# Layer 0's last output projection: seven half-depth products per pair of row blocks on two of three column chunks

## The chip, the cores and the metric

The kernel runs on one core of a Trainium2 chip. The metric is the time of one execution on the device in microseconds (us). Five engines matter: TensorE (PE: the matmuls, and PEld: their weight loads), VectorE (DVE), ScalarE (ACT), GpSimd (POOL) and SyncE (SP), which issues most of the DMAs. Each engine runs its own instructions in the order of the program and waits on semaphores for the others.

## The reference, cut to what matters

The program is one inference step of a two-layer decoder trunk over 1024 prompt tokens and 32 sample tokens (1056 columns in all). Layer 0 is a recurrent block, layer 1 a gated linear recurrence.

```
xn = rmsnorm(x); u = xn @ w_in                  # layer 0, 1024 -> 2 * 1536
xb, gate = u[..., :1536], u[..., 1536:]
h  = rg_lru(causal_conv(xb))                    # recurrence over the tokens
y  = h * silu(gate)                             # 1536 rows
x1 = x + y @ w_out                              # 1536 -> 1024: the change is in here
...
layer 1 begins with rmsnorm(x1)                 # so it needs every row of x1 in a column
```

## The kernel before

Activations lie with the features on the 128 partitions and the 1056 tokens along the columns, cut into three chunks of 352 columns (0, 1, 2). Every f32 matrix product is made in three matmuls (`mm3`, L245 to L249): each operand is split into a high part that the PE's reduced f32 form holds exactly and a low part with the rest, and high x high, high x low and low x high are summed in PSUM. ACT makes a high part by a cast, DVE or POOL makes a low part by a subtraction. A block of weights is 128x128, so one block on one chunk costs three matmuls of 128x352.

The 1536 rows of y come in four groups of three blocks. `out(g)` adds the product of groups 0 and 1 to x in DRAM. The last two groups are taken together by `out_last` (L660): for every chunk and each of the eight row blocks m of the result it forms one product over six blocks of y, three of group 2 (`ycols`, the tiles yh and yl) and three of group 3 (`xcols`, the tiles xh and xl). That is 18 matmuls to one PSUM bank; a DVE addition (L710) then adds x, a DMA writes the row block of x1, ACT squares it and POOL adds the squares (`squares`). After the eight blocks of a chunk, `norm` sums the squares over the partitions by a small matmul, POOL takes the power, DVE writes a diagonal and a second matmul spreads the factor; `scaled_parts` (L470, L471, L335) then makes layer 1's high and low parts. The norm and the scaling of chunk c run while the PE is on chunk c+1, those of chunk 2 while the PE is on the first products of layer 1 (`first1`).

The weights of `out_last` stay in the core for all three chunks. `load` fetches them by 128x384 pieces into the small tiles wraw, ACT casts (L670), POOL subtracts (L671), and the parts lie in room that has become free: row block 4 in the gate tiles gh and gl, row blocks 0 to 3 in X (the inputs of the recurrence), 5 to 7 in the last 256 columns of xh and xl and in the tiles whi and wlo.

What y needs first: the last gate products, two row blocks on three chunks (`gate(3, (1, 2), True)`, the DVE lines L534 and L535), and `split_y` (L627 to L632), which makes the high and low parts of groups 2 and 3 by an ACT cast and a DVE subtraction with two inputs in SBUF.

The order of the work is not written out by hand. All operations of the layer go as a list into `Flow`, which holds a duration for each, plans them forwards and backwards, and emits every engine's instructions in the planned order. Operations marked `main` keep their written order on the PE. On the chip the emitted order is fixed.

## Time and profile before

| what | value |
|---|---|
| median of 3 runs | 1046.37 us (1045.69 to 1050.2) |
| profiled execution: time, span of its instructions | 1044.86 us, 1043.1 us |
| mean granted TensorE clock | 0.997 |
| PE busy, matmuls | 98% of the span, 10264 |
| DVE, ACT, POOL busy | 73%, 65%, 48% |

A row of the timeline gives the start in us from the span's first instruction, the busy time, the engine, the line of the kernel, the operation, the output and inputs by the program's names, and how many were merged ("x2"); in square brackets stands the idle time before it and what ended that. The recorded busy times of two neighbours overlap a little, so the pitch of a run is the distance of the starts. `out_last` begins on the PE at 413.68 us.

### The profile page before, as it was taken

To read this page: it belongs to the slowest core of one execution; us is meant where nothing else is said; L and a number is where in the kernel's file an instruction comes from. 1 tells how busy PE (TensorE), PEld (TensorE's weight loads), DVE (VectorE), ACT (ScalarE), POOL (GpSimd) and SP (SyncE) were. 2 spreads that over 40 slices of the span, in tenths; PEclk is the share of its full clock that TensorE was granted. 3 is DMA by queue.
4 is the path that set the end of the run, shared out by engine and by line. 5 is a ranking of instruction groups with operands and counts; after the bars stand their busy time and mean duration, and the time that the engine had idled before them with its cause. 6 is when DMAs were issued, how large, how long until landed. Compare 5 with 4: busy or idle time off the path is not lost.

```text
span 1043.1 us, 26196 instructions
## 1 busy us (share of the span) xinstructions
PE 1027.3 (98%) x10264; PEld 1006.9 (97%) x10264; DVE 756.4 (73%) x1465; ACT 678.6 (65%) x1534; POOL 501.7 (48%) x526
## 2 busy tenths in 40 slices
PE   9999999999999999999999999999999999999996
PEld 9999999999999999999999999999999999999995
DVE  7999997788888599346687555554657567899656
ACT  6568656966865776333468686767777685786444
POOL 3425343444535265645754555555545353244554
PEclk9999999999999999999999999999999999999998
DMA  9201112123752586435676666566567571765554
GB/s 306 64 16 58 54 48 74 41 73 87 228 185 59 154 278 195 152 104 188 209 185 158 124 153 126 145 125 164 120 150 185 137 183 65 227 180 122 108 112 167
DMA packets 90764, 143.71 MB, mean 138 GB/s; under 512 B 11152, under 2 KB 56592, under 8 KB 90640
## 3 DMA queue, kind: packets, MB, share of 16 engines
q1 hardware_dynamic: 74656, 112.46, 34.2%
q0 software_dynamic: 13680, 26.81, 15.2%
q10 hardware_dynamic: 2304, 2.77, 0.8%
q8 instruction: 80, 1.31, 0.5%
q14 instruction: 44, 0.36, 0.1%
HBM read 81.60 MB, written 33.05 MB: 110 GB/s over the span
## 4 chain that ended last, share of the span: by engine, by line
PE 91%; DVE 5%; DMA 2%; issue 1%; POOL 0%; ACT 0%; POOLq 0%; ACTq 0%; DVEq 0%
PE mm L247 26%; PE mm L248 25%; PE mm L249 25%; PE hg L1063 2%; PE hg L1174 1%; PE hg L1281 1%; PE hg L579 1%; PE hg L1235 1%; PE hg L1283 1%; PE hg L247 1%; PE hg L248 1%; PE hg L249 1%; DMA wraw<-in_w_dram 1%; PE hg L1325 1%; DVE R L445 1%
## 5 line engine op out<-in xcount | busy, mean ns | idle before, releaser
L247 PE MATMUL mm<-xh,whi 128*128 128x352 f32 (+1 forms) x1147 | 353.8, 308 | 1.8 <-DVE sg L1543 1.8
L248 PE MATMUL mm<-xl,whi 128*128 128x352 f32 (+1 forms) x1147 | 348.6, 304 | 0.0
L249 PE MATMUL mm<-xh,wlo 128*128 128x352 f32 (+1 forms) x1147 | 348.4, 304 | 0.0
L247 PEld LDWEIGHTS mm<-xh,whi 128*128 128x128 f32 x1147 | 215.5, 188 | 4.1 <-DVE sg L1543 2.2
L248 PEld LDWEIGHTS mm<-xl,whi 128*128 128x128 f32 x1147 | 215.7, 188 | 1.5 <-DVE xl L335 0.2
L249 PEld LDWEIGHTS mm<-xh,wlo 128*128 128x128 f32 x1147 | 215.6, 188 | 0.0
L335 POOL TENSOR_TENSOR wlo<-wraw,whi 128x512 fp32r<-128x512 f32 (+1 forms) x62 | 89.9, 1458 | 82.8 <-ACT whi L390 74.2
L247 PE MATMUL mm<-t,whi 128*128 128x264 f32 x408 | 118.3, 290 | 0.0
L249 PE MATMUL mm<-t,wlo 128*128 128x264 f32 x408 | 115.8, 284 | 0.5 <-POOL wlo L335 0.5
L248 PE MATMUL mm<-t,whi 128*128 128x264 f32 x408 | 115.7, 284 | 0.0
L511 DVE SCALAR_TENSOR_TENSOR k<-xb,prm_sb,k 128x352 f32<-128x352 f32 (+2 forms) x144 | 90.0, 636 | 11.0 <-ACT k L508 7.8
L247 PEld LDWEIGHTS mm<-t,whi 128*128 128x128 f32 x408 | 76.8, 188 | 0.9
L249 PEld LDWEIGHTS mm<-t,wlo 128*128 128x128 f32 x408 | 76.6, 188 | 0.7 <-POOL wlo L335 0.7
L248 PEld LDWEIGHTS mm<-t,whi 128*128 128x128 f32 x408 | 76.9, 188 | 0.1
L322 POOL DMA_DIRECT2D wlo<-wraw x52 | 45.5, 874 | 64.6 <-ACT wlo L321 44.9
L1543 DVE TENSOR_TENSOR k<-mm,k 128x264 f32<-128x264 f32 x72 | 30.7, 429 | 58.7 <-PE mm L249 55.3
L594 POOL TENSOR_TENSOR k<-X 128x352 f32<-128x352 f32 x36 | 43.7, 1224 | 48.0 <-DVE R L595 38.8
L322 POOL DMA_DIRECT2D wlo<-R x32 | 29.4, 926 | 45.1 <-ACT wlo L321 36.5
L247 PE MATMUL mm<-yh,whi 128*128 128x352 f32 x153 | 49.9, 326 | 0.0
L249 PE MATMUL mm<-yh,wlo 128*128 128x352 f32 x153 | 49.4, 323 | 0.0
L248 PE MATMUL mm<-yl,whi 128*128 128x352 f32 x153 | 49.4, 323 | 0.0
L390 ACT CAST whi<-wraw 128x512 fp32r<-128x512 f32 (+1 forms) x63 | 36.3, 591 | 20.0 <-DMA wraw<-in_w_dram 7.7
(425 smaller groups left out, 2680.8 us busy)
## 6 DMA issues: line engine op xcount, KB each, us to landing
wraw<-in_w_dram SPq DMA_DIRECT2D x88, 256.0 KB, 3.3
wlo<-wraw POOLq DMA_DIRECT2D x49, 256.0 KB, 4.1
wlo<-R POOLq DMA_DIRECT2D x30, 256.0 KB, 4.1
wraw<-in_wo_dram SPq DMA_DIRECT2D x37, 192.0 KB, 3.0
ysum<-sg SPq DMA_DIRECT2D x9, 528.0 KB, 5.1
si<-in_s_in_dram SPq DMA_DIRECT2D x8, 512.0 KB, 4.0
R<-in_w_dram SPq DMA_DIRECT2D x16, 256.0 KB, 3.4
out_ss_out_dram<-si SPq DMA_DIRECT2D x8, 512.0 KB, 3.0
```

The costliest lines, as they stand in the source:

```text
L247: T.matmul(out, wh, xh, start=first, stop=False, skip_group_check=chained)
L248: T.matmul(out, wh, xl, start=False, stop=False, skip_group_check=chained)
L249: T.matmul(out, wl, xh, start=False, stop=last, skip_group_check=chained)
L322: fl.add("POOL", 0.93, lambda: G.dma_start(dst.bitcast(F32), src, accum_op=ALU.add), (*r, *w), w, prio, n / 2)
L335: emit = lambda: e.tensor_tensor(b, x, a.bitcast(F32), op=ALU.subtract)
L390: act(m, lambda hi=hi, raw=raw, m=m: S.copy(hi[:, :m], raw[:, :m]), rk, (hk,), prio)
L445: (pool if e is G else dve)(CH, lambda: e.tensor_tensor(a[:, :CH], a[:, :CH], sq, op=ALU.add), (sk, ak), (ak,), 2)
L511: dve(u, lambda src=src, dst=dst, sh=sh, k=k: V.scalar_tensor_tensor(dst, sh(src, k), pc("cw", 12 * k + m), dst, op0=ALU.mult, op1=ALU.add ...
L579: fl.add("PE", 0.62, lambda ps=ps, i=i, c=c: T.matmul(ps[:96, :CH], gs[:, i, :], ST[:96, chunk(c)], start=True, stop=True), (("gs",), *((" ...
L594: pool(CH, lambda x=x, a=a, b=b: G.tensor_tensor(x, a.bitcast(F32), b.bitcast(F32), op=ALU.add), (ak, bk), (xk,), 3)
L1063: T.matmul(ps[32 * j:32 * j + 32, n * w:n * w + w], B[:, o:o + 32], q(slice(o, o + 32)), start=True, stop=True, tile_position=(0, 32 * j))
L1543: dve(QT, lambda: V.tensor_tensor(o[0], z[0], u[0], op=ALU.add), (z[1], u[1]), (o[1],), 0)
```

## The change

On chunks 0 and 1 the eight row blocks are taken as four pairs (m, n) = (0,1), (2,3), (4,5), (6,7). The weights of a pair, two row blocks by two halves of three blocks (11 and 12 for m, 21 and 22 for n), and the y of the two chunks by two groups make a 2x2 by 2x2 product. It is formed by seven products of half the depth (9 matmuls of 128x352 each) in place of eight. The steps, by the kernel's numbers, and where each sum lies in PSUM (a, b, c are three banks of a pair):

```
weights: s = 21 + 22; 21 = 21 - 11; 11 = 11 - s; 12 = 12 + 11        # combos, DVE, four per pair
y: t1 = y2[1]-y2[0]; t3 = y2[1]-y3[1]; t2 = t3-y2[0]; t4 = t2+y3[0]  # difference, DVE, once
step 1: a  = 11 (plain) * y2[0]     step 2: b  = 12 (plain) * y3[0]
step 5: c  = s  * t1                step 3: c += 12 * y3[1]
step 6: a += 11 * t2                step 7: a += 21 * t3
step 4: a += 22 (plain) * t4
```

After each step DVE adds the bank's sum so far to one row block of x1 (L799), so a later step on the same bank has to wait until that addition has read it. On the PE the steps of neighbouring pairs are interleaved: 1 and 5 of the first pair, then for each pair 2, 3, 6, step 1 of the next pair, 7, step 5 of the next pair, 4. In the last pair one plain product of chunk 2 (row block 6) stands between steps 6 and 7, and 7 and 4 follow each other. Then come the other seven products of chunk 2, formed as before. The norms of chunks 0 and 1 are both taken behind the last step.

The weights are now fetched whole, 128x768 a row block, into the tile R (four homes, used twice each), and cast from there (L681, L682). The combined weights and the differences of y are new DVE operations (L733, L759), and their high and low parts new ACT casts (L745, L764) and new DVE subtractions (L746, L765). Chunk 1 of group 2 is no longer split by itself, since only t1 is used of it.

```
-        def split_y(g):
-            for c in range(NCH):
+        def split_y(g, cs=range(NCH)):
+            for c in cs:
...
+            def combos(m, n):
...
+                both_("s", "21", "22", ALU.add)
+                both_("21", "21", "11", ALU.subtract)
+                both_("11", "11", "s", ALU.subtract)
+                both_("12", "12", "11", ALU.add)
+                return at_
+
+            def split(i, p):
+
+                (hi, hk), (lo, lk) = spot[p]
+                x, xk, kx = made[i][{5: "s", 3: "12", 6: "11", 7: "21"}[p]]
+                act(U, lambda: S.copy(hi, x), (xk, *kx), hk, 2)
+                dve(U, lambda: V.tensor_tensor(lo, x, hi.bitcast(F32), op=ALU.subtract), (xk, *kx, *hk), lk, 2, True)
+                return hi, lo, (*hk, *lk)
...
+            def difference(o, x, y, op):
+
+                (o, ok), (x, xk), (y, yk) = o, x, y
+                dve(CH, lambda: V.tensor_tensor(o, x, y, op=op), (xk, yk), (ok,), 2, True)
...
+                for (q, c) in {1: [(m, 0)], 2: [(m, 0)], 5: [(n, 1)], 3: [(m, 1)], 6: [(m, 1)], 7: [(n, 1)], 4: [(n, 0)]}[p]:
+                    if p in (1, 5, 3, 4):
+                        begin_x(q, c)
+                    add(q, c, ps, pk)
+                    if p in (2, 6, 7, 4):
+                        end_x(q, c, accs[c])
...
+            ready(0)
+            step(0, 1)
+            step(0, 5)
+            for i in range(4):
+                if i:
+                    step(i - 1, 4)
+                for p in (2, 3, 6):
+                    step(i, p)
+                if i < 3:
+                    ready(i + 1)
+                    step(i + 1, 1)
+                    step(i, 7)
+                    step(i + 1, 5)
+                else:
+                    whole_(last[0])
+                    step(i, 7)
+                    step(i, 4)
+            for c in range(2):
+                scaled(c, accs[c], range(KD))
+            for m in last[1:]:
+                whole_(m)
+            scaled(2, acc2, last)
...
-        split_y(2)
+        split_y(2, (0, 2))
```

Where the instructions stand now is shown at three places. First the PE at the start of the stage, before: behind the last gate product (bank mm_160) comes the product of row block 4, with weights in gh and gl that were made long ahead; yh0 to yh2 and yl0 to yl2 are group 2, xh and xl group 3.

```order
L249 MATMUL mm_160<-xh_108,wlo_130 128x352
L247 MATMUL mm_157<-yh0_151,gh_116 128x352
L248 MATMUL mm_157<-yl0_154,gh_116 128x352
L249 MATMUL mm_157<-yh0_151,gl_117 128x352
L247 MATMUL mm_157<-yh1_152,gh_116 128x352
L248 MATMUL mm_157<-yl1_155,gh_116 128x352
```

The same place now, from the end of step 1 of the first pair (bank mm_157) into step 5 (bank hg_164), whose weights are the parts whi_125 and wlo_129 of s.

```order
L249 MATMUL mm_157<-yh2_153,X_143 128x352
L247 MATMUL hg_164<-yh0_151,whi_125 128x352
L248 MATMUL hg_164<-yl0_154,whi_125 128x352
L249 MATMUL hg_164<-yh0_151,wlo_129 128x352
L247 MATMUL hg_164<-yh1_152,whi_125 128x352
L248 MATMUL hg_164<-yl1_155,whi_125 128x352
```

So the third matmul of step 5, the twelfth of the stage, reads a low part that DVE makes from s.

The second place is DVE behind the gate products. Before, the last gate product's two operations (L534 on mm_160, L535) were followed by the end of the recurrence, a few low parts and the first additions to x1:

```order
L534 SCALAR_TENSOR_TENSOR k_85<-k_85,mm_160 128x352
L535 SCALAR_TENSOR_TENSOR sg_150<-sg_150,k_85 128x352
L610 TENSOR_TENSOR R_73<-R_73,t0_119 128x8
L611 MEMSET a_113 128x8
L615 SCALAR_TENSOR_TENSOR R_73<-a_113,R_73 128x352
L710 TENSOR_TENSOR sg_146<-mm_157,sg_146 128x352
```

Now the same two are followed by the addition behind step 1 (L799 on mm_157), one difference (L759) and one low part of t1 (L765), and then by these rows:

```order
L759 TENSOR_TENSOR sg_148<-sg_145,sg_148 128x352
L765 TENSOR_TENSOR xl_101<-sg_148,xh_100 128x352
L765 TENSOR_TENSOR yl2_156<-k_85,yh2_153 128x352
L765 TENSOR_TENSOR xl_101<-sg_145,xh_100 128x352
L765 TENSOR_TENSOR xl_107<-sg_148,xh_106 128x352
L759 TENSOR_TENSOR sg_149<-sg_146,sg_149 128x352
L759 TENSOR_TENSOR sg_146<-sg_149,sg_146 128x352
L759 TENSOR_TENSOR sg_149<-sg_146,sg_149 128x352
L765 TENSOR_TENSOR xl_103<-sg_149,xh_102 128x352
L765 TENSOR_TENSOR xl_103<-sg_146,xh_102 128x352
L733 TENSOR_TENSOR R_73<-R_73 128x384
L746 TENSOR_TENSOR wlo_129<-wraw_121,whi_125 128x384
```

The low part of s (the last row) stands behind nine operations on t2, t3 and t4, which only steps 6, 7 and 4 read, and behind a combination of weights.

The third place is the PE at the end of the last pair: step 7 ends and step 4 begins, on the same bank mm_159 (xh_100 to xh_104 hold t3, xh_106 and xh_108 t4).

```order
L247 MATMUL mm_159<-xh_104,whi_126 128x352
L248 MATMUL mm_159<-xl_105,whi_126 128x352
L249 MATMUL mm_159<-xh_104,wlo_130 128x352
L247 MATMUL mm_159<-xh_106,whi_124 128x352
L248 MATMUL mm_159<-xl_107,whi_124 128x352
L249 MATMUL mm_159<-xh_106,wlo_128 128x352
```

Between the two steps there is no other work on the PE; in the earlier pairs step 5 of the next pair stands there. Before, neighbouring products always went to different banks.

More of the change, by code (lines that the diff above doesn't have):

```diff
@@ new lines, in split @@
+            def split(i, p):
[4 more added lines that the diff above has]
+                return hi, lo, (*hk, *lk)
+            t2 = [(xh[3 + j][:, chunk(1)], xl[3 + j][:, chunk(1)], (("xh", 3 + j, 1), ("xl", 3 + j, 1))) for j in range(3)]
@@ new lines, in out_last, with begin_x, add, end_x @@
+            accs = [next(xbs) for _ in range(2)]
+            count = [0, 0, 0]
+            def begin_x(m, c):
+                x, xk = place[m, c]
+                dma(x, src[m][:, chunk(c)], ((2, m, c),), (xk,), 3)
+            def add(m, c, ps, pk):
+                x, xk = place[m, c]
+                dve(CH, lambda: V.tensor_tensor(x, ps[:, :CH], x, op=ALU.add), (pk, xk), (xk,), 0)
+            def end_x(m, c, acc):
+                x, xk = place[m, c]
+                dma(x1d[m][:, chunk(c)], x, (xk,), (("x1d", m, c),), 3)
+                squares(count[c], x, xk, acc)
+                count[c] += 1
@@ new lines, in out_last, with ready @@
+            made = {}
+            def ready(i):
+                keep(two[i][0])
+                keep(two[i][1])
+                made[i] = combos(*two[i])
+            acc2 = next(xbs)
+            ready(0)
[11 more added lines that the diff above has]
+                    step(i + 1, 5)
+                else:
+                    whole_(last[0])
+                    step(i, 7)
+                    step(i, 4)
```

134 lines of the change are left out of this document (99 added, 35 removed).

## The prediction

> **What bounds the kernel now.** I read the page first, its table of busy time and the chain that ended last.
>
> ```profile
> PE 1027.3 (98%) x10264; PEld 1006.9 (97%) x10264; DVE 756.4 (73%) x1465; ACT 678.6 (65%) x1534; POOL 501.7 (48%) x526
> PE 91%; DVE 5%; DMA 2%; issue 1%; POOL 0%; ACT 0%; POOLq 0%; ACTq 0%; DVEq 0%
> ```
>
> The PE is busy nearly always and is 91% of the chain. So a matmul less is time gained, as long as nothing makes the PE wait. Next the stretches before and in the stage that changes (windows, 394 to 414, 414 to 456 us):
>
> ```profile
> core 0: us, PE busy (x) PEld busy (x) DVE busy (x) ACT busy (x) POOL busy (x), PEclk, DMA share, GB/s
> 394.00:414.00 20.00, 20.00 (x128) 20.00 (x126) 18.95 (x28) 11.85 (x27) 11.21 (x13) 1.00 0.60 193
> 414.00:456.00 42.00, 42.00 (x265) 42.00 (x264) 14.44 (x32) 12.99 (x29) 22.27 (x25) 1.00 0.40 128
> ```
>
> In the 20 us ahead of the stage DVE is 95% busy (18.95 of 20.00); in the stage it has much room (14.44 of 42.00). The PE has no gap in either. The change puts its new DVE work on the border of the two, and the question is whether DVE gets it done in time there.
>
> **The removed matmuls.** The PE's timeline where the first and the second product of chunk 0 begin:
>
> ```profile
> 413.52 0.32 PE L249 MATMUL mm<-xh,wlo 128*128 128x352 f32 x1
> 413.68 0.32 PE L247 MATMUL mm<-yh,gh 128*128 128x352 f32 x1
> ...
> 416.56 0.32 PE L247 MATMUL mm<-yh,X 128*128 128x352 f32 x1
> ```
>
> 18 matmuls take 2.88 us, so one is 0.160 us. Before, two chunks take 2 x 8 x 18 = 288; now 4 pairs x 7 steps x 9 = 252. 36 less: **-5.76 us**, all on the path. A step is 1.44 us.
>
> **The wait at step 5.** Time counts from T0 = 413.68, when step 1 of the first pair begins. Without waits step 5 begins at T0+1.44 and its third matmul, which needs the low part of s, at T0+1.76. How long are DVE's operations? Its timeline before, around this place, with POOL's beside it:
>
> ```profile
> 389.93 0.95 DVE L632 TENSOR_TENSOR yl<-sg,yh 128x352 fp32r<-128x352 f32 x2
> ...
> 403.57 0.52 DVE L632 TENSOR_TENSOR xl<-sg,xh 128x352 fp32r<-128x352 f32 x1
> 404.00 1.33 DVE L535 SCALAR_TENSOR_TENSOR sg<-sg,k 128x352 f32<-128x352 f32 x1
> ...
> 407.59 0.49 DVE L534 SCALAR_TENSOR_TENSOR k<-k,mm 128x352 f32<-128x352 f32 x1
> 408.01 0.52 DVE L632 TENSOR_TENSOR yl<-sg,yh 128x352 fp32r<-128x352 f32 x1
> 408.44 1.35 DVE L535 SCALAR_TENSOR_TENSOR sg<-sg,k 128x352 f32<-128x352 f32 x1
> 409.71 1.77 DVE L632 TENSOR_TENSOR yl<-sg,yh 128x352 fp32r<-128x352 f32 x2
> 411.41 0.51 DVE L534 SCALAR_TENSOR_TENSOR k<-k,mm 128x352 f32<-128x352 f32 x1
> 412.02 0.76 DVE L535 SCALAR_TENSOR_TENSOR sg<-sg,k 128x352 f32<-128x352 f32 x1
> 412.71 2.21 DVE L632 TENSOR_TENSOR xl<-sg,xh 128x352 fp32r<-128x352 f32 x3
> 414.84 0.52 DVE L632 TENSOR_TENSOR yl<-sg,yh 128x352 fp32r<-128x352 f32 x1
> 415.27 0.51 DVE L534 SCALAR_TENSOR_TENSOR k<-k,mm 128x352 f32<-128x352 f32 x1
> ```
>
> ```profile
> 403.57 2.64 POOL L671 TENSOR_TENSOR X<-wraw,X 128x384 fp32r<-128x384 f32 x2
> ...
> 408.01 2.66 POOL L671 TENSOR_TENSOR X<-wraw,X 128x384 fp32r<-128x384 f32 x2
> 411.39 2.27 POOL L671 TENSOR_TENSOR X<-wraw,X 128x384 fp32r<-128x384 f32 x2 [0.71 <-ACT X L670]
> ```
>
> Undisturbed, an operation has a pitch of 0.43 us (403.57 to 404.00), with one input in PSUM as well (407.59 to 408.01: 0.42). But the L535 at 404.00, which reads two SBUF tensors and meets a POOL subtraction begun at 403.57, takes 1.33. From 407.59 to 415.27 DVE makes 11 operations, 4.73 us at 0.43, in 7.68: 2.95 us more, over four POOL subtractions, so each POOL subtraction costs DVE 0.74 us.
>
> What DVE must do between T0 and the low part of s is in the order: L534 on the last gate product, L535, the addition behind step 1, and 14 more (five differences, seven low parts of t1 to t4, one combination and the low part of s itself): 17 operations, 7.3 us. The first needs ACT's tanh of the last gate product:
>
> ```profile
> 413.88 0.47 ACT L533 ACTIVATE k<-mm 128x352 f32<-128x352 f32 x1 [1.54 <-PE mm L249]
> 414.24 0.48 ACT L631 CAST xh<-sg 128x352 fp32r<-128x352 f32 x1
> ```
>
> It ends at T0+0.67, so DVE ends at T0+8.0 if nothing else holds it. ACT is in order too: its cast of the third block of t1 is the eighth of its instructions behind that tanh (0.48 each, some waiting for DVE) and ends at about T0+4.6, 0.8 us after DVE gets there; the casts for t4 and t3 cost some 0.6 more. **Lower end: T0+9.4, a wait of 7.7 us.** Above it lies POOL. The eight subtractions into X (now L682) come later than before, since R, where the weights land, becomes free only when the recurrence is done with it: by ACT's order four of the casts ahead of them stand between the tanh of the fourth gate product of this group and that of the last one, and three behind it. Seven at 0.74 is 5.2; 1.0 of that is absorbed where DVE waits for the last tanh. **Upper end: T0+13.6, 11.9 us.** I take **10.0**: the rows above show that such a collision costs nearly what an exclusive use would, but some of it falls into DVE's waits for ACT. What is queued behind the wait is the whole main chain on the PE, which has no other work; DVE, ACT and POOL run on and build up a lead, so I expect no second wait of this size: steps 2 to 7 find their parts ready or within a few tenths.
>
> **The clock behind the wait.** The PE's windows at the end of the kernel, where it runs dry:
>
> ```profile
> 1034.00:1036.00 2.00, 1.08 (x8) 1.00 1.01 364
> 1036.00:1038.00 2.00, 0.00 (x0) 0.54 1.02 366
> 1038.00:1040.00 2.00, 0.00 (x0) 0.50 1.01 339
> ```
>
> Two to three us without matmuls and the granted clock is 0.50. A wait of 10 us is longer, so the matmuls behind it may start at half rate. If the low clock stays as long as it took to come (2 to 3 us), it costs 1 to 1.5 us; if it returns at once, nothing. I take **+1.0**. [...]
>
> **Steps on one bank.** The additions to x1 in the stage, before:
>
> ```profile
> L710 DVE TENSOR_TENSOR sg<-mm,sg 128x352 f32<-128x352 f32 x13 | 6.8, 522 | 24.8 <-PE mm L249 24.8
> ...
> 422.55 0.52 DVE L710 TENSOR_TENSOR sg<-mm,sg 128x352 f32<-128x352 f32 x1 [1.06 <-PE mm L249]
> 425.45 0.52 DVE L710 TENSOR_TENSOR sg<-mm,sg 128x352 f32<-128x352 f32 x1 [2.38 <-PE mm L249]
> ```
>
> The third product's last matmul starts at 413.68 + 3 x 2.88 - 0.16 = 422.16; the addition starts 0.39 later and ends 0.91 after that matmul began. Step 4 of the last pair follows step 7 on one bank with nothing between: 0.91 less the pitch 0.16, and about 0.1 to wake the PE: **+0.85**. In the other pairs step 1 or 5 of the next pair (1.44) covers the 0.91 with 0.5 to spare, which a DVE operation held by POOL (1.33 above) can use up: six such places, 0 to 0.8 each, so 0 to 4.8; DVE's load there, per pair seven additions and eight two-input operations, is 15 x 0.43 = 6.5 of 10.1 us, so I take **+0.5** in all.
>
> **Hidden at no cost.** The weights' DMAs are 384 KB each; landing takes by these rows 3.0 us for 192 KB and 5.1 for 528 KB, so about 4.2.
>
> ```profile
> ysum<-sg SPq DMA_DIRECT2D x9, 528.0 KB, 5.1
> wraw<-in_wo_dram SPq DMA_DIRECT2D x37, 192.0 KB, 3.0
> ```
>
> The second use of a home can be fetched when the combinations and low parts of the pair in it are made, a whole pair (10.1 us) before its first step; if that cover went, about 4 us per pair would show. The norms of chunks 0 and 1 now share the seven plain products of chunk 2, 7 x 2.88 = 20.2 us, in place of one chunk each:
>
> ```profile
> L470 DVE SCALAR_TENSOR_TENSOR sg<-sg,prm_sb,hg 128x352 f32<-128x352 f32 x8 | 4.2, 571 | 0.1
> ```
>
> Sixteen of these at 0.49 pitch, 12 low parts and 7 additions at 0.43 are 16 us of DVE; chunk 0 is needed at the end of the 20, chunk 1 one product of layer 1 (24 x 0.16 = 3.8 us) later. It fits; with POOL's collisions 0 to 3 us could show, and I count none.
>
> **The sum.** -5.76 + 10.0 + 1.0 + 0.85 + 0.5 = +6.6 against the profiled execution's 1044.86 us (its span 1043.1 and 1.8 around it): 1051.5. The median of the runs shown is 1.5 us above that execution, so **1053 us**. About 0.5%, 5.2 us, is what a measurement of this kernel can tell from no change.
>
> **The rivals.**
>
> *DVE is ahead in time.* If POOL's subtractions fall elsewhere and ACT's casts run early, s could be split before T0+1.76. For it: DVE idles in the stage before. Against: the order puts 17 operations there, two of which wait for the last gate product and one for step 1 itself. Then -5.76 + 0.85 + 0.5 = -4.4, **1042 us**, which is inside 0.5%; with no hand-over costs 1040.6. Chance 0.2, half of it on the faster side of 0.5%.
>
> *Half the wait.* DVE reaches s by about T0+6, if waits overlap better than I add them up: 4.3 us, the clock falls little, and gain and loss cancel: **1046.5 us**. Against: 7.3 us of DVE work alone is more than that. Chance 0.15.
>
> [...] Chance 0.1.
>
> The wait as summed has the chance 0.55, with its own range from -5.76 + 7.7 + 0.85 = +2.8 to -5.76 + 11.9 + 1.5 + 0.85 + 2 = +10.5, so 1049 to 1057.
>
> **How the numbers follow.** Range 1041.5 to 1059. Slower by over 0.5% (above 1051.6): three fifths of the 0.55, rounded up to 0.4, the 0.1 of the shared interface, and 0.03 for small new waits elsewhere, since the planner rearranges the whole layer: 0.53. Faster by over 0.5% (below 1041.1): 0.1. The same: 0.37.
>
> **What would show it.** In the changed kernel's PE waits one line of some 10 us in the stage, on a low part of weights from DVE, at the third matmul of the first step 5; a granted clock below 1.00 just behind it; 36 matmuls less; about 0.9 us at the last step 4. DVE without idle time up to the low part of s. Wrong would be: no wait above 3 us at the start of the stage, or waits of 1 us and more spread over all four pairs.

## The result, and the profile after

The changed kernel takes **1065.55 us** (median of 6 runs, 1062.11 to 1069.88), the kernel before, beside it, 1045.93 us (6 runs, 1044.49 to 1050.2). The ratio is 1.0169, 95% interval 1.0142 to 1.0197: slower, by 19.6 us between the medians. The prediction was 1053, with a range up to 1059: the direction was right, and the size was too small by 12.5 us. The profiled execution took 1066.38 us (before: 1044.86), its span is 1064.6 us (before: 1043.1), 21.5 us more.

The first two lines that answer to those of before, from the page: its table of busy time, and the chain that ended last.

```profile
PE 1030.9 (97%) x10228; PEld 1007.4 (95%) x10228; DVE 795.3 (75%) x1530; ACT 687.5 (65%) x1559; POOL 502.1 (47%) x526
PE 48%; DVE 5%; DMA 2%; POOL 1%; issue 1%; ACT 0%; POOLq 0%; DVEq 0%; SPq 0%; ACTq 0%
```

The 36 matmuls are gone (10264 to 10228). The PE's share of the chain fell from 91% to 48%, but that is not the loss: the shares add up to 57%, since the chain can be followed back only to 447.43 us, where it runs out on DVE. It does not reach the stage's first steps, so what happened there is read from the PE's own waits.

The windows of the same two stretches, moved by the 4.77 us by which the stage now begins later:

```profile
core 0: us, PE busy (x) PEld busy (x) DVE busy (x) ACT busy (x) POOL busy (x), PEclk, DMA share, GB/s
398.77:418.77 20.00, 20.00 (x125) 20.00 (x124) 18.49 (x35) 7.96 (x20) 7.63 (x12) 1.00 0.32 99
418.77:460.77 42.00, 30.86 (x174) 29.99 (x173) 38.51 (x66) 20.89 (x49) 19.55 (x19) 0.84 0.46 141
```

In the stage DVE went from 14.44 to 38.51 us of 42, and the PE from 42.00 to 30.86 at a clock of 0.84. The PE's timeline shows where; the last row is the first matmul of layer 1's recurrence, which serves as a landmark below.

```profile
418.45 0.33 PE L247 MATMUL mm<-yh,X 128*128 128x352 f32 x1
...
421.43 0.43 PE L247 MATMUL hg<-yh,whi 128*128 128x352 f32 x1 [1.36 <-ACT whi L745]
...
431.27 0.66 PE L249 MATMUL hg<-yh,wlo 128*128 128x352 f32 x1 [9.26 <-DVE wlo L746]
...
447.49 0.43 PE L249 MATMUL hg<-xh,wlo 128*128 128x352 f32 x1 [0.52 <-DVE wlo L746]
...
462.31 0.40 PE L247 MATMUL mm<-xh,whi 128*128 128x352 f32 x1 [0.40 <-DVE sg L799]
...
476.41 0.43 PE L247 MATMUL mm<-xh,whi 128*128 128x352 f32 x1 [0.62 <-DVE sg L799]
...
536.94 0.25 PE L1228 MATMUL hg<-R,a 128*32 128x64 f32 x2
```

The wait of 9.26 us stands at the third matmul of the first step 5, on the low part of s, and 1.36 us on ACT's cast of s stands just ahead of it. Only three small waits follow in the stage. Why the low part of s comes so late shows on DVE, whose timeline has no idle time here (L534 at 420.92 is the first operation on the last gate product), and on POOL beside it:

```profile
418.67 1.34 DVE L759 TENSOR_TENSOR k<-sg 128x352 f32<-128x352 f32 x1
...
420.92 0.52 DVE L534 SCALAR_TENSOR_TENSOR k<-k,mm 128x352 f32<-128x352 f32 x1
...
424.87 1.32 DVE L765 TENSOR_TENSOR yl<-k,yh 128x352 fp32r<-128x352 f32 x1
426.11 1.75 DVE L765 TENSOR_TENSOR xl<-sg,xh 128x352 fp32r<-128x352 f32 x2
427.78 1.63 DVE L759 TENSOR_TENSOR sg<-sg 128x352 f32<-128x352 f32 x3
...
430.67 0.55 DVE L746 TENSOR_TENSOR wlo<-wraw,whi 128x384 fp32r<-128x384 f32 x1
```

```profile
418.26 1.36 POOL L682 TENSOR_TENSOR X<-R,X 128x384 fp32r<-128x384 f32 x1 [1.39 <-ACT X L681]
...
422.25 1.01 POOL L682 TENSOR_TENSOR X<-R,X 128x384 fp32r<-128x384 f32 x1 [2.63 <-ACT X L681]
...
424.70 2.34 POOL L682 TENSOR_TENSOR X<-R,X 128x384 fp32r<-128x384 f32 x2 [1.44 <-ACT X L681]
```

An operation alone has a pitch of 0.43 to 0.47 us; the 1.34 and 1.32 are two of those that meet one of these four POOL subtractions. The low part of s ends at about 431.2, 12.8 us after the stage began.

What the clock does behind the wait, in the windows:

```profile
422.00:424.00 2.00, 0.02 (x1) 0.00 (x0) 2.00 (x5) 1.27 (x4) 1.01 (x1) 0.75 0.09 30
424.00:426.00 2.00, 0.00 (x0) 0.00 (x0) 2.00 (x4) 1.76 (x5) 1.26 (x2) 0.50 0.02 4
...
434.00:436.00 2.00, 2.00 (x8) 2.00 (x8) 2.00 (x6) 0.88 (x3) 0.00 (x0) 0.50 0.18 64
436.00:438.00 2.00, 2.00 (x13) 2.00 (x12) 0.50 (x2) 0.09 (x1) 0.00 (x0) 0.84 0.88 241
```

The granted clock falls to one half at 422.99 and stays there until 436.64, 13.65 us in all, the last 5.3 of them after the PE has begun again. 18 matmuls start at 0.29 us from each other (the first after 0.46) in place of 0.16: 2.5 us lost. In the other runs the clock came back 2.9 to 6.2 us after the PE had begun again (2.9 us in "no POOL low parts" and "one early product", 3.2 us in "two early products" with own banks, 6.2 us in "places of before, 36 matmuls"). In all profiles of this study a half clock inside the run lasted 3.4, 6.8, 10.2 or 13.7 us, multiples of 3.41. What decides between these lengths no run shows.

**Where the 21.5 us are.** The landmark stood at 521.40 in the kernel before:

```profile
521.40 0.26 PE L1063 MATMUL hg<-R,a 128*32 128x64 f32 x4
```

So three stretches can be compared: up to the stage's first matmul (413.68 to 418.45, **+4.77**), from there to the landmark (107.72 to 118.49, **+10.77**), and from the landmark to the end (521.7 to 527.7, **+6.0**). The prediction's sum has +6.6 for the second stretch and nothing for the other two. The second was the easy one. In the other two the PE's matmuls are the same, and in layer 1 all instructions even stand in the same order on every engine.

### The profile page after: what moved, and what is told of

Its sections match the earlier page's. It is cut to its first block, busy times and chain, and to the rows that moved or that the text cites. A ratio compares the mean times of both kernels' runs of the same rounds, so it can differ in the third digit from the quotient of the medians.

```text
span 1064.6 us, 26216 instructions
## 1 busy us (share of the span) xinstructions
PE 1030.9 (97%) x10228; PEld 1007.4 (95%) x10228; DVE 795.3 (75%) x1530; ACT 687.5 (65%) x1559; POOL 502.1 (47%) x526
## 4 chain that ended last, share of the span: by engine, by line
PE 48%; DVE 5%; DMA 2%; POOL 1%; issue 1%; ACT 0%; POOLq 0%; DVEq 0%; SPq 0%; ACTq 0%
PE mm L247 13%; PE mm L248 12%; PE mm L249 12%; PE hg L1228 2%; PE hg L1446 1%; PE hg L1339 1%; PE hg L1448 1%; DVE R L1210 1%; PE hg L1400 1%; DMA wraw<-in_wo_dram 1%; DMA a<-xn 1%; DVE a L1412 1%; PE hg L1490 1%; DVE t L335 0%; DVE sg L1210 0%
## 5 line engine op out<-in xcount | busy, mean ns | idle before, releaser
L247 PE MATMUL mm<-xh,whi 128*128 128x352 f32 (+2 forms) x1166 | 360.6, 309 | 5.6 <-DVE sg L1708 4.0
L248 PE MATMUL mm<-xl,whi 128*128 128x352 f32 (+2 forms) x1166 | 355.8, 305 | 0.0
L249 PE MATMUL mm<-xh,wlo 128*128 128x352 f32 (+2 forms) x1166 | 355.6, 305 | 0.0
L247 PEld LDWEIGHTS mm<-xh,whi 128*128 128x128 f32 x1166 | 219.2, 188 | 9.1 <-DVE sg L1708 5.1
L248 PEld LDWEIGHTS mm<-xl,whi 128*128 128x128 f32 x1166 | 219.7, 188 | 1.4
L249 PEld LDWEIGHTS mm<-xh,wlo 128*128 128x128 f32 x1166 | 219.3, 188 | 0.0
L575 ACT ACTIVATE R<-hg,smalls 128x352 f32<-128x352 f32 x72 | 38.0, 552 | 18.5 <-DVE R L615 15.5
```

Source lines behind the costliest of these rows:

```text
L247: T.matmul(out, wh, xh, start=first, stop=False, skip_group_check=chained)
L248: T.matmul(out, wh, xl, start=False, stop=False, skip_group_check=chained)
L249: T.matmul(out, wl, xh, start=False, stop=last, skip_group_check=chained)
L575: act(CH, lambda ps=ps, R=R, i=i, j=j, hb=hb, m=m: S.activation(R[:, i, j], ps[:, :CH], AF.Tanh, bias=hb[:, m:m + 1], scale=0.5), (pk, ("s ...
```

## The experiments

The table has the three stretches for every run, from the profiled execution of each, and the PE's pauses in layer 1 that the profile puts down to no wait (it calls what ended them "issue"). "Ratio" is to the kernel before, on the same chip, with its 95% interval; runs without one were executed once. The single executions took 1070.64 us (changed, again), 1044.72 (before, again), 1063.21 (no POOL low parts), and 1041.66, 1060.27 and 1056.37 (the three without POOL sums, in the table's order).

| kernel | stage begins | stage | layer 1 | pauses in it | span | median, ratio |
|---|---|---|---|---|---|---|
| before | 413.68 | 107.72 | 521.7 | 0.5 | 1043.1 | 1045.93 |
| before, again | 413.20 | 107.72 | 522.1 | 0.6 | 1043.0 | |
| before, changed places | 416.32 | 108.04 | 522.8 | 0.3 | 1047.2 | 1050.92, 1.0044 (1.0024 to 1.0065) |
| before, delayed by 9.6 | 422.90 | 108.03 | 526.4 | 0.6 | 1057.3 | 1059.23, 1.0126 (1.0108 to 1.0145) |
| before, no POOL sums | 413.42 | 107.72 | 518.5 | 0.6 | 1039.6 | |
| changed | 418.45 | 118.49 | 527.7 | 2.5 | 1064.6 | 1065.55, 1.0169 (1.0142 to 1.0197) |
| changed, again | 419.69 | 118.53 | 530.6 | 4.2 | 1068.8 | |
| s first | 418.29 | 118.23 | 527.9 | 1.8 | 1064.4 | 1066.79, 1.0177 (1.0143 to 1.0211) |
| order by need | 419.49 | 125.24 | 524.9 | 3.2 | 1069.6 | 1075.33, 1.0253 (1.0219 to 1.0287) |
| no POOL low parts | 418.86 | 113.82 | 528.4 | 4.3 | 1061.1 | |
| 56 matmuls in the wait | 418.64 | 117.69 | 520.1 | 0.6 | 1056.4 | 1061.52, 1.0122 (1.0091 to 1.0152) |
| places of before | 414.99 | 118.12 | 524.8 | 3.2 | 1057.9 | 1060.09, 1.0133 (1.0114 to 1.0151) |
| two early products | 420.10 | 117.51 | 527.4 | 4.8 | 1065.0 | 1063.80, 1.0172 (1.0150 to 1.0194) |
| the same, own banks, places of before | 416.63 | 117.70 | 524.5 | 3.8 | 1058.8 | 1060.42, 1.0133 (1.0104 to 1.0162) |
| one early product, places of before | 416.46 | 119.40 | 524.7 | 2.2 | 1060.6 | 1061.70, 1.0147 (1.0123 to 1.0172) |
| changed, no POOL sums | 417.51 | 118.14 | 522.8 | 4.9 | 1058.4 | |
| the same, 36 matmuls in the wait | 417.97 | 118.31 | 518.3 | 0.0 | 1054.6 | |
| places of before, 36 matmuls | 415.40 | 118.66 | 521.5 | 1.5 | 1055.6 | 1057.61, 1.0103 (1.0068 to 1.0138) |

### The wait in the stage

My theory was "load": DVE is the bound from the stage's first matmul to 434 us, with all that it must make for the first pair, and the order within that load moves the wait without shortening it. The rival: the low part of s merely stands too far back in DVE's order.

**s first.** Two operations of the planned order are moved, nothing else: ACT's cast of s, and DVE's low part of s, to about 10 us earlier. The list says behind which operation each one is put.

```
-        fl.moves = []
+        fl.moves = [(('xc', 1, 3), [('cast', 0, 5)]),      # ACT: cast of s behind the last cast into X for row block 1
+                    (('diff', 2, 0), [('low', 0, 5)])]     # DVE: low part of s behind the first t2
```

> The changed kernel with two instructions moved, all else in the same order: the cast of s comes on ACT behind the cast for row block 1's second half, and the low part of s on DVE ahead of the last gate product's operations, 14 places earlier. Theory A (order): only the low part of s is late, because it stands behind work that steps 6, 7 and 4 need. Then the PE's waits at the start of the stage fall from 11 us to 4 or less (the third block of t1 is next), the half clock shrinks, and the ratio to before falls from 1.017 to about 1.008. Theory B (load): DVE has too much to do here whatever the order; step 5 runs some 5 us earlier, but step 3 and step 6 then wait for their weights' low parts, which come no earlier than now (15 and 17 us behind the start of step 1). Then the sum of the PE's waits in the first 30 us of the stage falls by 3 us at most, and the ratio stays at 1.013 to 1.016.

The low part of s now costs 1.15 us of waiting. The PE's timeline (in this kernel `mm3` has the lines L273 to L275, the low part of s L780, those of the differences L802, the additions to x1 L837):

```profile
421.39 0.43 PE L275 MATMUL hg<-yh,wlo 128*128 128x352 f32 x1 [1.15 <-DVE wlo L780]
...
424.12 0.43 PE L274 MATMUL hg<-yl,whi 128*128 128x352 f32 x1 [2.15 <-DVE yl L802]
...
426.23 0.66 PE L274 MATMUL hg<-yl,whi 128*128 128x352 f32 x1 [1.18 <-DVE yl L802]
...
433.98 0.63 PE L273 MATMUL hg<-xh,whi 128*128 128x352 f32 x1 [4.15 <-DVE xo L837]
```

One wait of 9.26 has become four, 8.63 us in all, each for the next thing on DVE, and the stage takes 118.23 us in place of 118.49. With the 1.36 us on ACT's cast, which is gone, the waits in front fell by 2.0 us, from 10.62 to 8.63: "load" had expected 3 us at most and holds, and the rival falls. The ratio, 1.0177, is still a little above the 1.013 to 1.016 that "load" gave.

**Order by need.** 38 operations of DVE and 23 of ACT, of the first pair, are put in the order in which the PE's steps use them (the same list, longer).

> The changed kernel with DVE's and ACT's operations at the start of the stage put in the order in which the steps need them: step 5 (s, t1), step 3 (the combinations, the low part of 12), step 6 (t3 and t2, the low part of 11), step 7, step 4. The same operations, none left out. Theory A (order): nearly all of the 11 us of waits and the 2.4 us of half clock go, ratio 1.003 to 1.006. Theory B (load): about half is left, 4 to 6 us, spread over steps 5, 3 and 6, none as long as 9 us; the ratio is 1.007 to 1.011. Both say that it beats the one-move kernel.

Neither figure came: the stage is 6.8 us longer. In front the waits did fall, from 10.6 to 7.4 us, in four pieces with none above 4.0, so the order was worth about a third of them. But ACT's timeline and the PE's show a new one:

```profile
448.69 0.51 ACT L711 CAST gh<-R 128x384 fp32r<-128x384 f32 x1 [5.86 <-DMA R<-in_wo_dram]
```

```profile
452.85 0.66 PE L273 MATMUL hg<-xh,whi 128*128 128x352 f32 x1 [6.41 <-ACT whi L778]
```

In the new order the last reads of the first pair's homes in R came later, the weights of the third pair were fetched later, and ACT, in order, waited 5.86 us for them with the second pair's casts queued behind. The prediction had this cover as hidden "a whole pair" ahead, with about 4 us if it went. Here it goes, for 6.4.

**No POOL low parts.** POOL's four subtractions for row blocks 2 and 3 are left out; the low parts of those weights then hold what was there, so the kernel serves this measurement alone.

```
-                pool(u, lambda: G.tensor_tensor(lo, raw, hi.bitcast(F32), op=ALU.subtract), (*rk, a), (*lks, b), 1)
+                pool(u, (lambda: None) if m in (2, 3) else lambda: G.tensor_tensor(lo, raw, hi.bitcast(F32), op=ALU.subtract), (*rk, a), (*lks, b), 1)
```

> The changed kernel without POOL's four subtractions for row blocks 2 and 3 (their weights then have wrong low parts); all other instructions and their order as they were. If each POOL subtraction costs DVE 0.74 us, the low part of s comes 2.2 to 3.0 us earlier (from 12.7 us behind the start of step 1 to about 10). If DVE and POOL do not hurt each other, it comes at the same time.

```profile
428.15 0.66 PE L275 MATMUL hg<-yh,wlo 128*128 128x352 f32 x1 [6.81 <-DVE wlo L780]
```

The low part of s is there 9.3 us after the stage began in place of 12.8, and the stage is 4.7 us shorter. So these four subtractions made up 3.5 us of DVE's load ahead of s, 0.88 us each, more than the 2.2 to 3.0 expected: the collision term of the prediction is real. Its upper end had seven collisions at 0.74 (less 1.0), 4.2 us in all.

**56 matmuls in the wait.** Matmuls whose results are thrown away stand ahead of the first step 5, where the PE has nothing else to do.

```
+                    if (i, p) == (0, 5):
+                        for _ in range(56):
+                            T.matmul(ps[:, :CH], blocks[m][0][0], ycols(0)[0][0], start=True, stop=True, skip_group_check=True)
                     for j, ((wh, wl, _), (uh, ul, _)) in enumerate(zip(w, ops)):
```

> The changed kernel with 56 more matmuls of 128x352 (9 us) ahead of step 5, into the bank that step 5 then overwrites, so that the PE has something to do during its wait. If the wait's idleness is what halves the clock, the granted clock stays 1.00, the 18 matmuls behind the wait take 0.16 in place of 0.29 us, and the ratio falls by 0.002 (2.4 us). If the slow matmuls come from something else (DVE, POOL or DMA traffic), they stay slow. The wait itself ends when it did.

```profile
431.51 0.66 PE L275 MATMUL hg<-yh,wlo 128*128 128x352 f32 x1 [1.91 <-DVE wlo L780]
```

The low part of s comes when it came before (431.3), whatever the PE does meanwhile: DVE sets that time. The stage is only 0.8 us shorter, since behind the 1.91 us that were left unfilled the clock was at half once more, for 3.4 us (0.50 from 432 to 434 us, 0.76 to 436). But the span is 8.2 us shorter, and 7.6 of that lie in layer 1, which the edit doesn't touch. This opened the second question.

**Two early products**, the real work that could fill the wait: two plain products of chunk 2 between the first pair's steps 1 and 5.

```
             step(0, 1)
+            whole_(0)
+            whole_(1)
             step(0, 5)
...
-            for m in last[1:]:
+            for m in (7, 5, 4, 2, 3):
                 whole_(m)
```

> The changed kernel with two plain products of chunk 2 (row blocks 0 and 1, 36 matmuls, 5.8 us of PE work) taken from the end of the stage and put between step 1 and step 5 of the first pair; tiles at the addresses of the changed kernel. Theory 'load' (DVE is busy without a gap from step 1 to 434 us, so what the PE does meanwhile is free): the waits between step 1 and the low part of s shrink by 4 to 6 us, half clock costs 1 us less, and the time is 1058 to 1061. Rival 'end': less of chunk 2's plain work is left behind the last step, so the norms and scalings of chunks 0 and 1 are late for layer 1 by what was gained in front; then the time stays at 1064 to 1067, with a PE wait of 4 to 6 us at layer 1's first products.

(Two homes of x1 change places as well.) It took 1063.80 us, between the two forecasts. But in this kernel the second pair takes the two PSUM banks in which the first pair still sums, and it has waits on those banks. I made it again with banks of its own, and with the tiles where the kernel before has them (see below):

```
+            for _ in range(2):
+                next(mm)
             step(0, 5)
```

> The changed kernel with two plain products of chunk 2 (36 matmuls) between step 1 and step 5 of the first pair, now in PSUM banks of their own (two banks of the ring are passed over, so that the second pair does not take those of the first), and with the tiles at the addresses of the kernel before. Theory 'load': against the changed kernel at the addresses of before (1060.1) the waits ahead of step 5 shrink by 4 to 6 us and 1 us less of half clock follows; if nothing is lost at the other end, 1053 to 1055. Rival 'end': with two products less behind the last step, layer 1's first products wait 3 us more for the norms, as in the version with shared banks: then 1056 to 1058.

```profile
422.94 0.66 PE L248 MATMUL mm<-xl,X 128*128 128x352 f32 x1 [3.11 <-DVE xl L633]
...
431.77 0.43 PE L249 MATMUL hg<-yh,wlo 128*128 128x352 f32 x1 [2.60 <-DVE wlo L747]
```

The waits in front fell from 10.6 to 5.7 us, since also chunk 2's parts of y come from the loaded DVE; layer 1's first matmuls stood 5.1 us earlier. But 4.7 us of that were lost again before the landmark: with two products less behind the last step the PE waited 1.5 us for norms and scaled parts, and its clock from 500 to 520 us was 0.91 in place of 1.00. The stage (117.70) is 0.4 us shorter than without (118.12). The rival "end" came, with 4.7 in place of 3 us; the time, 1060.42, is that without the early products (1060.09), above both forecasts.

> As the version with two early products, but with one (row block 0, 18 matmuls, 2.9 us). Theory 'load': the waits ahead of step 5 shrink by 2.5 to 3 us, 1056.5 to 1058. Rival 'end': 1 to 1.5 us of it is lost again at layer 1's first products, 1058 to 1059.5.

With one early product the wait for chunk 2's part is as long (3.11), the one for s 5.60, and the end loses too: 119.40, no gain at all. Its 1061.70 us lie above both forecasts.

### Ahead of the stage: where the tiles lie

The matmuls of layer 0 are the same in both kernels, and yet from 100 to 250 us the changed kernel falls behind evenly. Windows of before, then of the changed kernel; the number behind PE's busy time counts its matmuls:

```profile
120.00:180.00 60.00, 60.00 (x377) 59.76 (x376) 51.45 (x97) 37.82 (x82) 25.62 (x33) 1.00 0.21 59
```

```profile
120.00:180.00 60.00, 60.00 (x372) 59.76 (x371) 54.46 (x100) 39.11 (x84) 25.26 (x33) 1.00 0.21 59
```

Without a gap and at a clock of 1.00, 377 matmuls fit in 60 us before and 372 after: 1.3% slower. In the built programs every instruction of these loops works on the same tiles, but 30 tiles lie at other SBUF addresses: a pool gives out its places in the order of first use, and the planner's new order changed that (the first high part of x at 33,856 bytes before, at 97,216 after). To tell places from order I swapped the places alone, by 24 one-column fills in front of everything; all else keeps its order.

```
+            for k_ in [("xh", 3), ("xh", 0), ("whi", 1), ("xl", 3), ...]:     # 24 tiles, in the other kernel's order of first use
+                G.memset(first_[k_][:, :1].bitcast(F32), 0.0)
             fl.run(SEARCH, 60.0)
```

> The kernel before, with its instructions in the same order, but 24 tiles (the high and low parts of the normalized input and of the streamed weights) put at the SBUF addresses that they have in the changed kernel, by 24 one-column memsets on POOL ahead of everything. Theory 'places': the pitch of the 352-column matmuls hangs on where the tiles lie; then the mean pitch from 120 to 240 us rises from 159.5 to about 161.7 ns, out_last starts at 418.0 to 418.8 us in place of 413.68, and the time is 4 to 6 us above before. Rival 'order': the 4.8 us come from the changed order of layer 0's instructions; then the pitch stays at 159.5 ns, out_last starts at 413.5 to 414.2, and the time is that of before, 1046 to 1048.

> The changed kernel with its instructions in the same order, but the same 24 tiles put at the addresses that they have in the kernel before. Theory 'places': pitch from 120 to 240 us about 159.5 ns, step 1 starts near 413.9 us in place of 418.45, the waits of the stage stay (9 to 11 us), the time is about 1061. Rival 'order': step 1 starts at 418.2 to 418.8, and the time stays at 1065 to 1067.

The same window of the kernel before with the changed places, and of the changed kernel with the places of before:

```profile
120.00:180.00 60.00, 60.00 (x372) 59.76 (x371) 51.14 (x97) 37.40 (x80) 25.07 (x33) 1.00 0.21 59
```

```profile
120.00:180.00 60.00, 60.00 (x377) 59.76 (x376) 55.02 (x100) 39.68 (x86) 25.27 (x33) 1.00 0.21 60
```

The counts go with the places and not with the order: shown. The stage begins 2.6 us later in the kernel before (416.32; 4.3 to 5.1 were expected) and 3.5 us earlier in the changed one (414.99); the whole time moves by +4.5 us (1050.92 against 1046.47 beside it) and by about -5.5 us (1060.09 against 1065.55, in different sets of runs). Of the 4.77 us ahead of the stage, 2.6 to 3.5 are thus the places, and the other 1.3 to 2.1 the new order (single gaps, one of about a microsecond at 287 us). Which property of an address makes a matmul slow I did not find.

### Layer 1: pauses, and how DVE and POOL fall

Layer 1's length is 521.7 in the kernel before and 520.1 to 528.4 in the changed kernel's versions up to here, with the same instructions in the same order. First, how fixed is it? Both kernels ran again, unedited, and the kernel before ran with 60 matmuls more in front of the stage (`for _ in range(60): T.matmul(...)` ahead of the first product).

> The changed kernel once more, not edited. Theory 'phase': same order and places, but layer 1's stretch (from the matmul that stood at 497 us to the end, 566 us in the first profile) comes out otherwise by 1 us or more, with PE waits on DVE at other places; the stage and all ahead of it agree within 0.5 us. Rival 'kernel': every part agrees within 0.5 us.

> The kernel before once more, not edited. Theory 'phase': out_last and all ahead of it within 0.5 us of the first profile, layer 1's stretch otherwise by 1 us or more. Rival 'kernel': every part agrees within 0.5 us.

> The kernel before with 60 matmuls of 128x352 more in front of out_last's first product, results thrown away (9.6 us of PE time; all else in the same order). Theory 'phase' (layer 1's length is not fixed: DVE's SBUF-only operations there are held up by POOL operations or not, by how the two engines happen to fall): layer 1 starts 8 to 9.6 us later, and its length changes by more than 1.5 us either way, up to the 6 us of the changed kernel; PE waits on DVE of 0.6 to 1.5 us come or go. Rival 'kernel' (layer 1's 5 to 6 us belong to the seven products): layer 1's length stays within 1 us of before, total 1054.5 to 1056.

It is not fixed. The kernel before did repeat, within 0.5 us in every stretch. But the changed kernel's second execution begins the stage 1.2 us later, agrees within 0.1 us in the stage, and then takes 2.9 us more; the kernel before, only delayed, takes 4.7 us more (526.4). The one wait that makes most of the second execution's difference, and the clock behind it:

```profile
561.59 0.59 PE L249 MATMUL mm<-t,wlo 128*128 128x264 f32 x1 [2.71 <-POOL wlo L335]
```

```profile
562.00:564.00 2.00, 2.00 (x11) 2.00 (x11) 1.65 (x4) 0.00 (x0) 1.27 (x2) 0.50 0.93 318
564.00:566.00 2.00, 2.00 (x11) 2.00 (x11) 0.00 (x0) 0.90 (x2) 0.00 (x0) 0.50 1.05 220
```

A low part from POOL is 2.7 us late, the clock stays at half for 6.1 us behind it, and 11 matmuls fit in 2 us. The same matmul waits 2.6 to 2.7 us in four of the 18 profiles, of both kernels; in the delayed kernel before it is the 2.74 us at 554.24, with 3.4 us of half clock behind. In the changed kernel's first execution the waits are on DVE instead. DVE's timeline of the changed kernel, POOL's beside it, and the PE's next matmul:

```profile
769.46 2.64 DVE L1210 TENSOR_TENSOR R<-R,sg 128x512 f32<-128x512 f32 x1
```

```profile
769.27 1.03 POOL L1371 TENSOR_TENSOR vb<-vst,bm 96x512 fp32r<-96x512 f32 x1
770.27 1.27 POOL L1635 TENSOR_TENSOR R<-R,wraw 128x512 f32<-128x512 f32 x1
```

```profile
772.49 0.39 PE L247 MATMUL mm<-xh,whi 128*128 128x264 f32 x1 [1.20 <-DVE sg L1708]
```

The same DVE operation in the kernel before, and another of its kind there:

```profile
751.34 0.81 DVE L1045 TENSOR_TENSOR R<-R,sg 128x512 f32<-128x512 f32 x1
...
806.70 2.74 DVE L1045 TENSOR_TENSOR R<-R,sg 128x512 f32<-128x512 f32 x1
```

The changed kernel's takes 2.64 us where two POOL operations run beside it and ends at 772.10, 0.56 us after the second of them (at 771.54); the addition that frees the PE's bank stands behind it. The kernel before has its own such case at 806.70, beside the same two kinds of POOL operation, with a PE wait of 1.50 us behind: both kernels meet these collisions, at different places. With no POOL operation beside it, as at 789.97 in the changed kernel, the operation takes 0.67 us.

To see what is left without such collisions, POOL's 56 two-input sums of weights in layer 1 (the expectations say 55) were replaced by fills of the same tiles, in both kernels, which then lack these sums and serve this measurement alone:

```
-                pool(512, lambda: G.tensor_tensor(o, x, y, op=op), (xk, yk), (ok,), 2)
+                pool(512, lambda: G.memset(o, 0.001), (xk, yk), (ok,), 2)
```

> The kernel before, but in layer 1 the 55 two-input additions and subtractions of weights on POOL are left out (a one-input fill of the same tile stands in their place, so the output is not the reference's). Theory 'POOL': the additions hold up DVE's SBUF-only operations (0.67 us alone, up to 2.74 us beside them) and come late themselves; without them layer 1 loses its waits of 0.5 to 1.5 us on DVE, its stretch (from the matmul at 482 us to the end, 561 us) gets shorter by 1 to 3 us, and that of the changed kernel, edited likewise, agrees with it within 1.5 us. Rival 'places and kernel': the stretches of the two edited kernels still differ by 4 to 7 us.

> The changed kernel with the same edit in layer 1. Theory 'POOL': its stretch of layer 1 (567.6 us in its first profile, 571.2 us in its second) gets shorter by 5 to 9 us and agrees with that of the kernel before, edited likewise, within 1.5 us; the two spans then differ by 14.5 to 17 us, which is the stage and what lies ahead of it. Rival 'places and kernel': it stays 4 to 7 us longer than that of the other, and the spans differ by 20 us or more.

Layer 1 got shorter in both, 521.7 to 518.5 and 527.7 (530.6) to 522.8, and the waits on DVE of 0.5 to 1.5 us went. But 4.3 us of difference stayed: theory "POOL" explains only a part. What stayed are pauses of the PE that are put down to no wait, 4.9 us against 0.6. Less these pauses layer 1 takes 517.9 us in both kernels, so the places, which still differ between the two kernels, cost layer 1 nothing that shows. Here are the pauses, in the PE's timeline of the changed kernel without the sums:

```profile
563.60 0.39 PE L247 MATMUL mm<-t,whi 128*128 128x264 f32 x1 [1.36 <-issue]
...
597.64 0.94 PE L1400 MATMUL hg<-sg,kt 128*128 128x128 f32 x6 [1.25 <-issue]
...
729.21 0.28 PE L249 MATMUL mm<-t,wlo 128*128 128x264 f32 x1 [0.87 <-issue]
...
877.22 1.05 PE L1400 MATMUL hg<-sg,kt 128*128 128x128 f32 x7 [1.41 <-issue]
```

They stand at the same places in the other versions with 36 matmuls less (564, 597, 730, 882 us and thereabouts, not every one in every run; three more stand elsewhere), and not in the kernel before, nor in the one with 56 matmuls in the wait. The DMA view of that kernel from 874.5 to 877.3 us, the time up to the last of the four, has a single packet:

```profile
q8 instruction: 1, 0.02, 2.7%
```

The profile calls what queue q8 carries "instruction": 80 packets of 16 KB in a span. In all 18 profiles of this study there are 46 such pauses in layer 1, and each ends 2.2 to 3.2 us after a packet of q8 began (44 of them 2.2 to 2.7). The kernel before has 20,600 recorded PE instructions (10,264 matmuls, as many weight loads, 72 of the sequencer); if all 80 packets of 16,384 bytes are the PE's, that is an estimated 63.6 bytes each, and 20,600 / 80 = 257.5 in a packet. And counted from the first PE instruction, each of the 46 pauses stands 193 or 194 past a multiple of 256 (193 at 691.81 in the kernel before; 194, 193 and 194 at 597.28, 730.98 and 882.21 in the changed one). So the pauses go with the count of PE instructions and with the packets of q8; that the PE has run out of instructions there and waits for the next packet is my reading of these figures. The packets start some 20 us apart among the long matmuls of layer 0 and 3 to 19 us apart in layer 1 with its short ones. If the count decides, the number of PE instructions ahead sets which of the short ones a pause falls on. That can be tried: 36 matmuls are put where the PE waits anyway (the edit of the 56, with 36), so that layer 1 stands at the same count as in the kernel before; once without POOL's sums, and once with nothing left out and the places of before.

> The changed kernel with POOL's layer-1 additions left out as in the two runs before, and 36 matmuls of 128x352 (results thrown away) ahead of the first pair's step 5, where the PE waits anyway, so that layer 1's PE instructions stand at the same count from the program's start as in the kernel before. Theory 'count' (the four pauses of the PE in layer 1 that no wait explains come where a certain number of PE instructions has been issued; the changed kernel has 36 matmuls less, so they fall on other instructions): the pauses named 'issue', 5.0 us without the 36, come down to 1 us or less, and layer 1's stretch agrees with that of the kernel before, edited likewise, within 1.5 us. Rival 'kernel': the four pauses stay at the same instructions with 2.4 to 5 us, and the stretch stays 4 to 6 us longer.

> The changed kernel, nothing left out, with the tiles at the addresses of the kernel before and the 36 matmuls ahead of the first pair's step 5. Theory 'count': against the same kernel without the 36 (1060.1) the half clock behind the wait costs 0.5 to 1 us less and the pauses 2 to 4 us less, so 1055 to 1057.5; what is left over the kernel before is then the wait, 9 to 10 us. Rival 'kernel': 1059 to 1060.5.

Without the sums the pauses went from 4.9 to 0.0 us, and layer 1 takes 518.3 us, that of the kernel before with the same edit 518.5. With nothing left out it takes 521.5, that of the kernel before 521.7, and of its two pauses the first stands where the kernel before has its only one (on `mm<-si,ab`, 0.50 us at 691.81 there); the second is of its own:

```profile
428.48 0.66 PE L249 MATMUL hg<-yh,wlo 128*128 128x352 f32 x1 [5.34 <-DVE wlo L747]
...
703.45 0.42 PE L1397 MATMUL mm<-si,ab 128*32 128x128 f32 x7 [0.49 <-issue]
...
818.82 0.39 PE L1427 MATMUL hg<-vb,kst 128*128 128x512 f32 x1 [1.02 <-issue]
```

Against the same kernel without the 36 matmuls the gain is 2.5 us (1060.09 to 1057.61), just short of the forecast, and it lies in layer 1 (524.8 to 521.5, of it 1.7 in pauses). The half clock behind the wait cost no less: it lasted 6.2 us behind the wait, against 5.6 without them.

In this last kernel nearly everything but the stage is back: it begins 1.7 us later than before, the stage is 10.9 us longer, and layer 1 0.2 us shorter, 12.5 us in all (1055.6 against 1043.1). It is the best version of the change that I found, 1.0103 (1.0068 to 1.0138) of the time before; none beats the kernel before.

## Why the prediction was wrong

The step that failed is its sum, "-5.76 + 10.0 + 1.0 + 0.85 + 0.5 = +6.6 against the profiled execution's 1044.86". It has terms for the stage alone, and the whole rest of the program was set to zero change; the text had seen that "the planner rearranges the whole layer" and gave "small new waits elsewhere" three chances in a hundred. The runs showed +4.77 us ahead of the stage and +6.0 behind it. Point by point:

- **The removed matmuls, -5.76.** Right: 36 less, at 0.160 us.
- **The wait at step 5, 10.0 in 7.7 to 11.9.** Right in place and cause: 1.36 for the cast and 9.26 for the low part of s, 10.6 us. "S first" shows that it is mostly load and not order; "no POOL low parts" shows POOL's share, 3.5 us. That the size came out so near is in part luck, since three of its terms were off and balanced. DVE came to the last gate product 2.5 us behind the stage's start and not 0.7, because four operations for the differences of y stood ahead of it. It never waited for ACT, where the sum had 1.4 us. And POOL's collisions were four at 0.88 in place of seven at 0.74. The 17 operations, 7.3 us, were right.
- **"I expect no second wait of this size".** Right: 0.52, 0.40 and 0.62 us follow, and no later pair has a longer one. No run shows an interface of DVE and POOL that bounds all four pairs, to which the forecast gives 0.1 and its range the upper end, 1059; what the runs showed of the two engines in the stage is four POOL subtractions ahead of s at 0.88 us each ("no POOL low parts"), and PE waits of 0.40 to 0.62 us in the later pairs. Step 4 of the last pair lost 0.77 us where +0.85 stood (its 0.1 for waking the PE stands on no row; the PE began 0.06 us after DVE's addition ended), step 7 of the third pair 0.56 where +0.5 stood, and step 3 of the second pair 0.79 for a low part from DVE, which had no term.
- **The clock behind the wait, +1.0 in 0 to 1.5.** Too small: it stayed at half for 5.3 us and cost 2.5. The assumption that failed is that the low clock lasts "as long as it took to come (2 to 3 us)".
- **Hidden: norms and weights.** Right for this order: no PE wait stands between the last step and the landmark. "Order by need" and the early products show what each costs when the cover goes, 6.4 and 4.7 us.
- These account for the stage: -5.76, +13.6 in the first pair's steps 1, 5, 2 and 3 (19.4 us in place of 5.8: the two waits and the half clock) and +2.1 for the three later waits make 9.9, and of the 0.9 us left 0.3 to 0.4 are the places (118.49 against 118.12, and 108.04 against 107.72). The prediction's +6.6 was short by 4.2, of which the clock is 1.5.
- **What had no term.** Places: 2.6 to 3.5 us ahead of the stage, shown by swapping them. Count of PE instructions: 2.0 us in the first profile, up to 4.3, shown by the 36 matmuls. How DVE and POOL fall in layer 1: the rest of its 6.0 us, some 4 in this profile (the PE's waits on DVE there went from 4.7 to 7.6 us), and as much as 4.7 in the kernel before when it was only delayed; shown as a cause by the runs without POOL's sums, but of no fixed sign. The new order ahead of the stage: 1.3 to 2.1 us, the remainder, not tested by a run of its own.

The range missed because it was made of the stage's unknowns. Even a stage predicted exactly, +10.8, would have given 1057 and left 8 us. The forecast that the change loses was right for the reason given: seven products save less (5.8 us) than the preparation of their operands on DVE delays the first of them (10.6 us).

What stays open: which property of an address slows a matmul, and how much of layer 1's length a given order would have on the average, for which one or two profiles of each kernel are too few.

## What to carry to other kernels

A saving on the engine that bounds the kernel must be set against the time at which its new operands are ready, and that time was here mostly a load on another engine, and not a place in its order: moving the late operation forward made the next ones late. An edit in a planned and packed program also changes what it does not touch: tile addresses, the count of PE instructions, with which the pauses went, and how the operations of DVE and POOL fall against each other, here 10.8 of 21.5 us; so compare the stretches ahead of and behind the edit before explaining anything by the edit. To measure the edit alone, put places and instruction count back, as the last kernel does.

## What the hardware showed that I had not expected

- The same matmuls at a clock of 1.00 without gaps ran 1.3% slower with other SBUF addresses (372 against 377 in 60 us), and the counts changed sides when the addresses were swapped (372 in "before, changed places", 377 in "places of before").
- Among short matmuls the PE paused 0.2 to 1.9 us with no wait on record, and went on 2.2 to 3.2 us after a 16 KB packet of queue q8 ("instruction") had begun; all 46 such pauses stand 193 or 194 PE instructions past a multiple of 256, and with 36 matmuls put back they went from 4.9 to 0.0 us (the two without POOL sums).
- What a wait of the PE costs in half clock behind it is not fixed. The 2.71 us at 561.59 cost 4.9 us in all against the first execution of the same kernel, behind the 1.91 us before 431.51 in "56 matmuls in the wait" it was at half for 3.4 us, and the 2.62 us before 547.73 in "before, changed places" left it at 1.00. Each time the clock was half inside a run, it was so for a multiple of 3.41 us (13.65 in the changed kernel's first profile).
- A DVE operation with two SBUF inputs took 2.64 us beside two POOL operations (at 769.46), 0.67 us alone (at 789.97); which of its kind met them changed from run to run.
